# Cross-covariance attention: reading the logits straight from the grams, with a matmul of ones to spread 1/|k|

## The chip, the core and the metric

The kernel runs on one core of one Trainium2 chip. The metric is the device time in microseconds (us) of one execution. The engines are named as in the profile: PE (TensorE), DVE (VectorE), ACT (ScalarE), POOL (GpSimd) and SP, which issues all the transfers here.

## What is computed

```python
batch, heads, seq, dim = 8, 12, 512, 64        # Q, K, V: float32
Q_norm = Q / (np.linalg.norm(Q, axis=-2, keepdims=True) + 1e-10)
K_norm = K / (np.linalg.norm(K, axis=-2, keepdims=True) + 1e-10)
attn = np.einsum('bhnd,bhne->bhde', Q_norm, K_norm)
attn = np.exp(attn - np.max(attn, axis=-1, keepdims=True))
attn = attn / (np.sum(attn, axis=-1, keepdims=True) + 1e-10)
return np.einsum('bhnd,bhde->bhne', V, attn).astype(np.float32)
```

For each of 96 heads the attention matrix is only 64 x 64: columns of Q against columns of K, each column scaled by the inverse of its norm over the 512 rows, then a softmax along the K columns, then V times that matrix.

## The kernel before

The 96 heads are worked on in 24 units of four heads. A unit's Q and K are two float32 tiles of 128 x 1024 (32 partitions to a head). `cast_q` and `cast_k` turn them into one bfloat16 tile `qkb` in which each row holds Q's 64 columns and then K's 64 columns. `grams` multiplies this tile with itself: 64 matmuls, in four row groups of PE, accumulate in PSUM (`gbuf`) for each head a 128 x 128 matrix. Its rows and columns 0 to 63 belong to Q, 64 to 127 to K. The diagonal therefore holds the squared norms, the upper right block Q^T K and the lower left block K^T Q.

`norms` (L115) reads the diagonal with four masked sums on DVE and raises it to the power -1/2 on POOL (L120, tile `rq`: the first 64 partitions hold 1/|q|, the other 64 hold 1/|k|). `keep_kq` (L108) copies K^T Q from PSUM to SBUF on ACT. `scale_k` (L125) multiplies its rows by 1/|k| on POOL. `logits` (L131) transposes the four heads' blocks on PE into the PSUM tile `lg`. `scale_q` (L135) multiplies the rows of the result, which are now Q's columns, by 1/|q| on DVE. `exps` and `normalise` make the softmax, and write the result into one of twelve zeroed bfloat16 tiles `abuf` (memsets at L213).

V goes another way. It is loaded for two units at a time, cast to bfloat16 (`cast_v`, L96), transposed on PE (`vtrans`, L155) and copied out by ACT (L159); the last four units skip the cast and are transposed as float32 (`vtrans_f32`, L170). `doubled` (L176) copies an attention matrix to the other 64 partitions by a matmul with the identity; `dup`, where it writes, shares a PSUM tile with `lg`. `outs` (L188) multiplies the transposed V with two heads' matrices at a time, and L192 copies the products to SBUF, from where SP stores them.

All loads and stores are on SP's queue, in the order in which the program issues them. Q and K have five buffers each, V four. The schedule is manual: what each engine does follows the order of the calls in the loop over s. Stage s issues the load of unit s+3, the grams, norms, copy and scale of unit s, the logits and exponentials of unit s-1 and the normalisation and doubling of unit s-2; the outputs follow at 0.9 units a stage. The PSUM tile of the grams has one buffer, so the grams of unit s+1 wait until the norms and the copy of unit s have read it. After the loop a tail of six steps makes the last six outputs, with the last unit's logits between them:

```python
        if i == 2:
            scale_q(last)
            exps(last)
        ...
        outs(u, both)
        if i == 1:
            logits(last)
```

Of the kernel before, what the change touches and what calls it, by code (L numbers as in the profile page):

```python
# [8 lines left out]
F32 = mybir.dt.float32  # L9
BF16 = mybir.dt.bfloat16  # L10
AF = mybir.ActivationFunctionType
ALU = mybir.AluOpType
AX = mybir.AxisListType

D = 64
HU = 4
# [11 lines left out]
def kernel(  # L28
# [7 lines left out]
    nc = tc.nc  # L36
    B, H, N, _ = Q.shape
# [9 lines left out]
    const = ctx.enter_context(tc.tile_pool(name="const", bufs=1))  # L47
# [6 lines left out]
    small = ctx.enter_context(tc.tile_pool(name="small", bufs=4))  # L54
# [7 lines left out]
    def outs_by(s):  # L62

        return max(0, (s - 2) * 9 // 10)


    qf, kf, vf, vb, qkb, nsq, rq, kqs, sl, ex, vt, so, kq = ({} for _ in range(13))

    def load_qk(u):
        qf[u] = qp.tile([128, R, D], F32, name="qf")  # L70
# [4 lines left out]
    def load_v(w):  # L75
        vf[w] = vp.tile([128, 2 * R * D], F32, name="vf")
        nc.sync.dma_start(out=vf[w], in_=Vf[w])

    def store(u, g=slice(0, SV)):
        nc.sync.dma_start(out=Of[u][:, g], in_=so[u][:, g].rearrange("p s t d -> p s (t d)"))  # L80
# [8 lines left out]
    def cast_v(v):  # L89

        w, i = divmod(v, 2)
        if i == 0:
            vb[w] = vbp.tile([128, A, TP, 2 * D], BF16, name="vb")
        x = vf[w].rearrange("p (a t d) -> p a t d", a=A, d=2 * D)
        for t, copy in ((2 * i, nc.scalar.copy), (2 * i + 1, nc.vector.tensor_copy)):
            copy(vb[w][:, :, t], x[:, :, t])  # L96
# [5 lines left out]
                x = qkb[u][NV * h:NV * (h + 1), t, :]  # L102
                nc.tensor.matmul(gbuf[:, h, 0:2 * D], x, x, start=(t == 0), stop=(t == R - 1), tile_position=(NV * h, 0))  # L103

    def keep_kq(u):

        kq[u] = small.tile([128, HU, D], F32, name="kq")
        nc.scalar.copy(kq[u][D:], gbuf[D:, :, 0:D])  # L108

    def norms(u):  # L110

# [7 lines left out]
        r = rq[u] = small.tile([128, HU], F32, name="rq")  # L119
        nc.gpsimd.tensor_tensor(out=r, in0=n2, in1=mhalf, op=ALU.pow)  # L120

    def scale_k(u):

        kk = kqs[u] = small.tile([128, HU, D], F32, name="kqs")
        nc.gpsimd.tensor_tensor(  # L125
            out=kk[D:], in0=kq[u][D:], in1=rq[u][D:, :, None].to_broadcast([D, HU, D]), op=ALU.mult,
        )

    def logits(u):
        for h in range(HU):  # L130
            nc.tensor.transpose(lg[:, h, :], kqs[u][D:, h, :], ident[D:, D:])  # L131

    def scale_q(u):
        s = sl[u] = small.tile([D, HU, D], F32, name="sl")
        nc.vector.tensor_tensor(out=s, in0=lg, in1=rq[u][0:D, :, None].to_broadcast([D, HU, D]), op=ALU.mult)  # L135

    def exps(u):
        e = ex[u] = small.tile([D, HU, D], F32, name="ex")
        nc.scalar.activation(e, sl[u], AF.Exp)  # L139

    def normalise(u):
        s = small.tile([D, HU], F32, name="esum")
        nc.vector.reduce_sum(out=s, in_=ex[u], axis=AX.X)
        ri = small.tile([D, HU], F32, name="rinv")
        nc.vector.reciprocal(ri, s)
        a = abuf[u % len(abuf)]
        nc.vector.tensor_tensor(out=a[0:D, :, 0, :], in0=ex[u], in1=ri[:, :, None].to_broadcast([D, HU, D]), op=ALU.mult)  # L147

    def vtrans(v):

        w, i = divmod(v, 2)
        ps = ps_v.tile([128, A, 2, 128], BF16, name="vps")
        for t in range(2):
            for a in range(A):
                nc.tensor.transpose(ps[:, a, t, :], vb[w][:, a, 2 * i + t, :], identb)  # L155

        if i == 0:
            vt[w] = vtp.tile([128, TP, 128, A], BF16, name="vt")
        nc.scalar.copy(vt[w][:, 2 * i:2 * i + 2], ps.rearrange("p a t c -> p t c a"))  # L159
# [13 lines left out]
    def doubled(u):  # L173

        a = abuf[u % len(abuf)]
        nc.tensor.matmul(dup[D:], identb[0:D, 0:D], a[0:D, :, 0, :], tile_position=(0, D))  # L176
        nc.scalar.copy(a[D:, :, 1, :], dup[D:])

    def outs(u, copies=(nc.scalar.copy, nc.scalar.copy)):
        s = so[u] = sop.tile([128, SV, TP, 2 * D], F32, name="so")  # L180
        a = abuf[u % len(abuf)]
        v = vt[u // 2][:, :, u % 2 * 64:(u % 2 + 1) * 64]
        for g in range(SV):
            po = ps_o.tile([128, TP, 2 * D], F32, name="po")
            for t in range(TP):
                for x in range(2):
                    h = 2 * g + x
                    nc.tensor.matmul(  # L188
                        po[MV * x:MV * (x + 1), t, :], v[:, t, NP * h:NP * (h + 1), :].rearrange("p c a -> p (c a)"),
                        a[:, h].rearrange("p a d -> p (a d)"), tile_position=(0, MV * x),  # L190
                    )
            copies[g](s[:, g], po)  # L192

    ps_g = main.enter_context(tc.tile_pool(name="ps_g", bufs=1, space=bass.MemoryType.PSUM))
    gbuf = ps_g.tile([128, HU, 512], F32, name="gram")
    ltile = ps_l.tile([128, 2, HU, D], F32, name="lgdup")
    lg = ltile[0:D, 0]
# [6 lines left out]
    ident = const.tile([128, 128], F32, name="ident")  # L204
# [2 lines left out]
    nc.gpsimd.tensor_copy(identb, ident)  # L207
    mhalf = const.tile([128, HU], F32, name="mhalf")
    nc.gpsimd.memset(mhalf, -0.5)
    abuf = []  # L210
    for i in range(12):
        a = const.tile([128, HU, 2, D], BF16, name=f"ab{i}")
# [3 lines left out]
    def on(f, u):  # L216
        if 0 <= u < U:
            f(u)
# [5 lines left out]
    for s in range(U):  # L224
        n0, n1 = outs_by(s - 1), outs_by(s)
        on(load_qk, s + LOAD_AHEAD)
        while nv < min(U, n1 + 5) // 2:
            load_v(nv)
            nv += 1
        while nst < n1 - 3:  # L230
            store(nst)
            nst += 1
        new = range(nt, n1 + 2) if s >= 1 else ()
        for v in new:
            cast_v(v)
        on(cast_q, s + 1)
        on(normalise, s - 2)
        on(grams, s)
        on(norms, s)
        on(keep_kq, s)  # L240
        on(scale_k, s)
        on(logits, s - 1)
        on(scale_q, s - 1)
        on(exps, s - 1)
        on(cast_k, s + 1)
        for v in range(n0, n1):
            outs(v)
        on(doubled, s - 2)
        for v in new:
            vtrans(v)  # L250
            nt = v + 1

    last = U - 1
# [4 lines left out]
    for i, u in enumerate(range(n1, U)):  # L258
        while nv < min(U, u + 6) // 2:
            load_v(nv)  # L260
            nv += 1
        store(u - 3)
        if i == 0:
            normalise(last - 1)
        if i == 2:
            scale_q(last)
            exps(last)
        if i == 3:
            normalise(last)
        on(vtrans_f32, u + 2)  # L270
        if i == 1:
            doubled(last - 1)
        if i == 3:
            doubled(last)
        outs(u, both)
        if i == 1:
            logits(last)
    for u in range(U - 3, last):
        store(u)
    for g in range(SV):  # L280
# [30 lines left out]
```

## Time and profile before

| | |
|---|---|
| time, median of 5 runs | 131.73 us (131.51 to 133.2) |
| profiled execution | 131.73 us, its span 130.0 us |
| busy share of the span | PE 69%, DVE 76%, ACT 65%, POOL 53% |
| DMA | 50.67 MB, mean 390 GB/s |
| mean granted TensorE clock | 0.823 of full speed |

The profile cuts the span in 40 slices of 3.25 us. Its chain of waits is followed back from the last instruction, each step to what released it. In a line of a group, the figures after the first bar are the busy time in us and the mean of one instruction in ns; those after the second are the idle time of the engine just before these instructions, and what ended most of it. In lines of the chain and of the timeline the first two numbers are the start and the length in us. Matrix products read "stationary columns, then moving operand", as "64*64 64x256".

### The profile page before, as it was taken

The numbers are of one execution on the slowest core, as the hardware profiler recorded it, in microseconds if no ns is written. First come the engines' busy times: TensorE is split into PE (matmuls) and PEld (weight loads), VectorE is DVE, ScalarE is ACT, GpSimd is POOL, SyncE is SP. The second block draws the span as 40 slices with busy tenths as digits, with TensorE's granted clock in tenths as the row PEclk, the third lists the DMA queues.
The fourth block names the chain that finished last, engine by engine and source line by source line (L and its number), as shares of the span: only waits on it lengthen the run. The fifth ranks groups of instructions, "written<-read, shape, count | busy, mean of one in ns | idle before, by whom it ended". The sixth has DMA issues, their size and how long they took to land.

```text
span 130.0 us, 5388 instructions
## 1 busy us (share of the span) xinstructions
PE 89.9 (69%) x2232; PEld 69.9 (54%) x2232; DVE 98.7 (76%) x366; ACT 84.8 (65%) x159; POOL 69.1 (53%) x68
## 2 busy tenths in 40 slices
PE   0044736779876988698966997759848966889630
PEld 0043634557655766486844685538627844668410
DVE  0774676898797989595899879797698498878740
ACT  3001375137799889875986379969759849987530
POOL 7924183688357755661588437727617718540000
PEclk9999995555999689655798569995995599999997
DMA  4999999999999999999999999999999999989784
GB/s 153 328 392 434 422 398 411 405 429 393 414 416 403 426 408 407 422 409 409 415 413 409 415 415 420 405 424 413 413 415 416 405 420 417 412 351 340 306 310 184
DMA packets 15208, 50.67 MB, mean 390 GB/s; under 512 B 1360, under 2 KB 1360, under 8 KB 13648
## 3 DMA queue, kind: packets, MB, share of 16 engines
q1 hardware_dynamic: 15184, 50.34, 97.1%
q8 instruction: 17, 0.28, 0.8%
q14 instruction: 7, 0.06, 0.1%
HBM read 37.75 MB, written 12.58 MB: 387 GB/s over the span
## 4 chain that ended last, share of the span: by engine, by line
PE 31%; DMA 26%; DVE 17%; ACT 9%; POOL 7%; issue 4%; SPq 2%; POOLq 0%; ACTq 0%; DVEq 0%
DMA vf<-in_V_dram 18%; PE gram L103 13%; DMA kf<-in_K_dram 9%; DVE scr L115 6%; PE po L188 6%; POOL rq L120 5%; PE vps L155 5%; PE lgdup L131 3%; ACT so L192 3%; PE vps L170 2%; ACT vt L159 2%; PE lgdup L176 2%; DVE qkb L84 2%; DVE qkb L87 2%; DVE sl L135 2%
## 5 line engine op out<-in xcount | busy, mean ns | idle before, releaser
L120 POOL TENSOR_TENSOR rq<-nsq,mhalf 128x4 f32<-128x4 f32 x24 | 47.6, 1983 | 44.0 <-DVE nsq L115 36.0
L103 PE MATMUL gram<-qkb 32*128 32x128 bf16 x1536 | 37.5, 264 | 14.4 <-DVE qkb L87 11.0
L103 PEld LDWEIGHTS <-qkb 32*128 32x128 bf16 x1536 | 31.1, 118 | 21.5 <-DVE qkb L87 14.1
L115 DVE CUSTOM_DVE_ANT_0 scr<-gram,ident 128x128 f32<-128x128 f32 x96 | 22.1, 284 | 11.7 <-PE gram L103 11.6
L108 ACT COPY kq<-gram 64x256 f32<-64x256 f32 x24 | 8.8, 367 | 30.5 <-DVE nsq L115 30.2
L192 ACT COPY so<-po 128x512 f32<-128x512 f32 x42 | 22.8, 588 | 1.6 <-PE po L188 1.0
L84 DVE CAST qkb<-qf 128x1024 bf16<-128x1024 f32 x24 | 19.8, 827 | 4.0 <-DMA qf<-in_Q_dram 4.0
L159 ACT COPY vt<-vps 128x1024 bf16<-128x1024 bf16 x20 | 20.2, 1012 | 1.2 <-PE vps L155 0.7
L188 PE MATMUL po<-ab,vt 128*64 128x128 bf16 x384 | 18.5, 242 | 2.0 <-ACT so L192 0.9
L155 PEld LDWEIGHTS <-vb 128*128 128x128 bf16 x160 | 11.7, 115 | 13.8 <-ACT kq L108 7.9
L155 PE MATMUL vps<-identb,vb 128*128 128x128 bf16 x160 | 15.8, 257 | 2.7 <-ACT vt L159 2.4
L188 PEld LDWEIGHTS <-vt 128*64 128x64 bf16 x384 | 13.5, 121 | 6.5 <-issue 4.0
L87 DVE CAST qkb<-kf 128x1024 bf16<-128x1024 f32 x24 | 16.2, 675 | 0.0
L125 POOL TENSOR_TENSOR kqs<-kq,rq 64x256 f32<-64x256 f32 x24 | 14.9, 621 | 1.9
L131 PE MATMUL lgdup<-ident,kqs 64*64 64x64 f32 x96 | 12.0, 259 | 4.7 <-POOL kqs L125 4.4
L176 PE MATMUL lgdup<-ab,identb 64*64 64x256 bf16 x24 | 7.4, 310 | 11.0 <-DVE sl L135 10.1
L96 ACT CAST vb<-vf 128x512 bf16<-128x512 f32 x20 | 12.3, 621 | 2.4 <-DMA vf<-in_V_dram 2.4
L96 DVE CAST vb<-vf 128x512 bf16<-128x512 f32 x20 | 8.5, 430 | 5.9 <-DMA vf<-in_V_dram 5.9
L131 PEld LDWEIGHTS lgdup<-ident,kqs 64*64 64x64 f32 x96 | 7.5, 128 | 8.9 <-POOL kqs L125 6.5
L139 ACT ACTIVATE ex<-sl 64x256 f32<-64x256 f32 x24 | 10.0, 417 | 2.0 <-DVE sl L135 1.2
L147 DVE TENSOR_TENSOR ab<-ex,rinv 64x256 bf16<-64x256 f32 x24 | 10.4, 432 | 0.8
L135 DVE TENSOR_TENSOR sl<-lgdup,rq 64x256 f32<-64x256 f32 x24 | 9.9, 412 | 1.1 <-PE lgdup L131 0.6
(20 smaller groups left out, 58.0 us busy)
## 6 DMA issues: line engine op xcount, KB each, us to landing
qf<-in_Q_dram SPq DMA_DIRECT2D x24, 512.0 KB, 11.3
kf<-in_K_dram SPq DMA_DIRECT2D x24, 512.0 KB, 11.2
vf<-in_V_dram SPq DMA_DIRECT2D x12, 1024.0 KB, 12.5
out_dram<-so SPq DMA_DIRECT2D x23, 512.0 KB, 11.3
out_dram<-so SPq DMA_DIRECT2D x2, 256.0 KB, 3.3
```

Source lines behind the costliest of these rows:

```text
L84: nc.vector.tensor_copy(qkb[u][:, :, 0:D], qf[u])
L87: nc.vector.tensor_copy(qkb[u][:, :, D:], kf[u])
L96: copy(vb[w][:, :, t], x[:, :, t])
L103: nc.tensor.matmul(gbuf[:, h, 0:2 * D], x, x, start=(t == 0), stop=(t == R - 1), tile_position=(NV * h, 0))
L115: nc.vector.tensor_tensor_reduce(out=scr, in0=gbuf[:, h, 0:2 * D], in1=ident, scale=1.0, scalar=1e-20, op0=ALU.mult, op1=ALU.add, accum_ou ...
L120: nc.gpsimd.tensor_tensor(out=r, in0=n2, in1=mhalf, op=ALU.pow)
L125: nc.gpsimd.tensor_tensor(out=kk[D:], in0=kq[u][D:], in1=rq[u][D:, :, None].to_broadcast([D, HU, D]), op=ALU.mult,)
L131: nc.tensor.transpose(lg[:, h, :], kqs[u][D:, h, :], ident[D:, D:])
L155: nc.tensor.transpose(ps[:, a, t, :], vb[w][:, a, 2 * i + t, :], identb)
L159: nc.scalar.copy(vt[w][:, 2 * i:2 * i + 2], ps.rearrange("p a t c -> p t c a"))
L188: nc.tensor.matmul(po[MV * x:MV * (x + 1), t, :], v[:, t, NP * h:NP * (h + 1), :].rearrange("p c a -> p (c a)"), a[:, h].rearrange("p a d ...
L192: copies[g](s[:, g], po)
```

## The change

The rows of the upper right block, Q^T K, already have the orientation that the softmax wants. `keep_qk` copies this block (partitions 0 to 63) instead of the lower left one. It goes into one of four constant tiles `qk`, whose partitions 64 to 127 hold an identity matrix for each head, written once at the start. `scale` multiplies all 128 partitions by `rq`: the upper half becomes Q^T K with its rows times 1/|q|, the lower half diagonal matrices of 1/|k|. `spread_k` multiplies a 64 x 64 block of ones with these diagonal matrices on PE, in float32, so that every row of `lg` holds 1/|k| along its columns. `logits` is now the elementwise product of `lg` and the scaled Q^T K on DVE. The four transposes are gone; in the order of the calls `spread_k` stands where `logits` stood, and `logits` where `scale_q` stood. At the start POOL writes the block of ones and the four identity tiles, ahead of the twelve memsets.

```diff
-    def keep_kq(u):
-
-        kq[u] = small.tile([128, HU, D], F32, name="kq")
-        nc.scalar.copy(kq[u][D:], gbuf[D:, :, 0:D])
+    def keep_qk(u):
+
+        nc.scalar.copy(qk[u % len(qk)][0:D], gbuf[0:D, :, D:2 * D])
...
-    def scale_k(u):
-
-        kk = kqs[u] = small.tile([128, HU, D], F32, name="kqs")
-        nc.gpsimd.tensor_tensor(
-            out=kk[D:], in0=kq[u][D:], in1=rq[u][D:, :, None].to_broadcast([D, HU, D]), op=ALU.mult,
-        )
+    def scale(u):
+
+        x = sc[u] = small.tile([128, HU, D], F32, name="sc")
+        nc.gpsimd.tensor_tensor(out=x, in0=qk[u % len(qk)], in1=rq[u][:, :, None].to_broadcast([128, HU, D]), op=ALU.mult)
+
+    def spread_k(u):
+
+        nc.tensor.matmul(lg, ones[D:], sc[u][D:], tile_position=(D, 0))
 
     def logits(u):
-        for h in range(HU):
-            nc.tensor.transpose(lg[:, h, :], kqs[u][D:, h, :], ident[D:, D:])
-
-    def scale_q(u):
         s = sl[u] = small.tile([D, HU, D], F32, name="sl")
-        nc.vector.tensor_tensor(out=s, in0=lg, in1=rq[u][0:D, :, None].to_broadcast([D, HU, D]), op=ALU.mult)
+        nc.vector.tensor_tensor(out=s, in0=lg, in1=sc[u][0:D], op=ALU.mult)
...
+    ones = const.tile([128, D], F32, name="ones")
+    nc.gpsimd.memset(ones, 1.0)
+    qk = []
+    for i in range(4):
+        x = const.tile([128, HU, D], F32, name=f"qk{i}")
+        nc.gpsimd.tensor_copy(x[D:], ident[D:, None, D:].to_broadcast([D, HU, D]))
+        qk.append(x)
     abuf = []
...
-        on(keep_kq, s)
-        on(scale_k, s)
+        on(keep_qk, s)
+        on(scale, s)
+        on(spread_k, s - 1)
         on(logits, s - 1)
-        on(scale_q, s - 1)
         on(exps, s - 1)
...
         if i == 2:
-            scale_q(last)
+            logits(last)
             exps(last)
...
         if i == 1:
-            logits(last)
+            spread_k(last)
```

More of the change, by code (lines that the diff above doesn't have):

```diff
@@ L64, in outs_by @@
         return max(0, (s - 2) * 9 // 10)
-    qf, kf, vf, vb, qkb, nsq, rq, kqs, sl, ex, vt, so, kq = ({} for _ in range(13))
+    qf, kf, vf, vb, qkb, nsq, rq, sc, sl, ex, vt, so = ({} for _ in range(12))
     def load_qk(u):
```

## The prediction

> **What bounds the kernel now.** I read the page's slices first, then its queues, then the chain of waits, then the timeline where the chain turns.
>
> ```profile
> PEclk9999995555999689655798569995995599999997
> DMA  4999999999999999999999999999999999989784
> GB/s 153 328 392 434 422 398 411 405 429 393 414 416 403 426 408 407 422 409 409 415 413 409 415 415 420 405 424 413 413 415 416 405 420 417 412 351 340 306 310 184
> ...
> q1 hardware_dynamic: 15184, 50.34, 97.1%
> ```
>
> From slice 3 to slice 35 the DMA engines are full at some 413 GB/s. A unit moves half a MB each of Q, K, V and output: 2.10 MB / 413 GB/s = 5.08 us of DMA. Per unit DVE is busy 98.7 / 24 = 4.1 us and PE 89.9 / 24 = 3.7 us. So up to about 104 us the transfers set the pace. In the last five slices the rate falls to 340, then 184: there the transfers wait for computation. Where one turns into the other stands in the chain of waits:
>
> ```profile
> 91.16 12.47 DMA vf<-in_V_dram
> 103.65 0.43 DVE vb L96
> ...
> 106.99 2.25 POOL rq L120
> 109.31 0.62 POOL kqs L125
> 109.98 0.41 PE lgdup L131 x4
> 110.39 0.57 PE po L188 x16
> ...
> 117.86 0.36 PE lgdup L131 x4
> 118.22 1.02 PE vps L170 x8
> ```
>
> At 103.65 VectorE stops waiting for V (it had sat idle 1.68 us for it). From there to the last copy, whose 0.69 us begin at 124.86, no step of the chain is a DMA. So what the change costs is read from these 22 us; before them a stage has 1 us to spare on DVE and the last wait forgives 1.68 us. The span is 130.0 us and this execution took 131.73, so 1.73 us lie around the span; 131.73 is also the median, so a sum against this execution is one against the median.
>
> **The change, part by part.**
>
> ```profile
> L155 PE MATMUL vps<-identb,vb 128*128 128x128 bf16 x160 | 15.8, 257 | 2.7 <-ACT vt L159 2.4
> L125 POOL TENSOR_TENSOR kqs<-kq,rq 64x256 f32<-64x256 f32 x24 | 14.9, 621 | 1.9
> L131 PE MATMUL lgdup<-ident,kqs 64*64 64x64 f32 x96 | 12.0, 259 | 4.7 <-POOL kqs L125 4.4
> L176 PE MATMUL lgdup<-ab,identb 64*64 64x256 bf16 x24 | 7.4, 310 | 11.0 <-DVE sl L135 10.1
> L135 DVE TENSOR_TENSOR sl<-lgdup,rq 64x256 f32<-64x256 f32 x24 | 9.9, 412 | 1.1 <-PE lgdup L131 0.6
> ```
>
> *Copy on ScalarE* (L108, 367 ns): the same 64x256 float32 from the same PSUM tile, other partitions and columns. Zero.
>
> *Multiply on VectorE* (L135, 412 ns): the same form; its second operand is a full 64x256 tile rather than a broadcast. It reads PSUM plus one SBUF operand before and after. Zero.
>
> *Scale on GpSimd* (L125): 64 partitions become 128, 256 elements in each. No row shows such a multiply on 128. The low end is the row, 0.62 us; the high end is time growing with partitions, 1.24 us. The Trainium skill (GPSIMD Engine Reference, Architecture) gives each of eight cores its own 16 partitions, all running the same instruction, which makes it 0.62 again. I take 0.62: zero. It is on the chain once, at 109.31; the other two late ones end at 112.27 and 115.64, before PE asks at 113.03 and 117.84. The high end thus costs 0.62 us once.
>
> *Matmul on PE.* Four float32 transposes of 64 columns go; one float32 matmul of 256 columns comes. The groups' means mix clocks, so I use the fastest instructions, as the tail runs at granted clock 1.00 from 112 us. In bfloat16, 128 columns take 213 ns (L103's minimum) and 256 take 265 ns (L176's): 0.41 ns a column on a fixed 0.16 us. In float32, transposes of 64 and 128 columns take 213 and 272 ns (minima of L131 and L170): 0.92 ns a column, twice as much. No float32 product stands in the trace. Three prices, with 256 columns:
> - as bfloat16 (the row of L176): 0.27 us;
> - at the rate of the float32 transposes: 0.16 + 256 x 0.92 ns = 0.39 us;
> - the Trainium skill (FP8 and Floating Point Precision, TensorE Precision Notes) speaks against the change: a true float32 product needs four passes through the array, every pairing of high and low halves. Estimate: 0.16 + 4 x 256 x 0.41 ns = 0.58 us; with three further weight loads uncovered, at 104 ns (L131's shortest), 0.89 us.
>
> The pieces in the chain are 0.41 us at 109.98 (unit 21) and 0.36 us at 117.86 (unit 23): 0.77 together. Two spreads cost 0.54, 0.78, 1.16 or 1.78 us, so the end moves by -0.23, 0.0, **+0.39** or +1.01. By the row nearest in shape the kernel gains a little; by the rule it loses. I take four passes, since [...] the row of L176 is not float32. Unit 22's spread (113.03) lies beside its norms: VectorE reads the result only at 113.72, and 113.03 + 0.58 = 113.61. It is covered by 0.1 us; at 0.89 it would cost 0.2 more.
>
> Queued behind the spread on PE are the output matmuls, the doubling matmul, the V transposes and the next grams. The doubling also waits for the VectorE multiply (10.1 us of L176's idle time), which comes after the norms: 0.84 us of norms and 0.41 of multiply against 0.58 + 0.64 of spread and output matmuls. These just match, so at full clock no new wait arises. Before, the weight load waited for GpSimd; now the weights are the constant ones and only the product waits. I give nothing for that.
>
> At half clock a spread is dearer: L176's slowest is 420 ns, L103's 310, so 0.86 ns a column on 0.20 us, and four passes make 1.08 us against some 0.63 for four transposes, +0.45 in a stage. Between 20 and 104 us the DMA's 5.08 us hide it; without that cover, see the third rival.
>
> *Prologue on GpSimd.*
>
> ```profile
> 1.64 5.59 POOL L213 MEMSET ab<- 128x512 bf16 x12
> 3.96 3.81 DVE L84 CAST qkb<-qf 128x1024 bf16<-128x1024 f32 x1 [3.96 <-DMA qf<-in_Q_dram]
> 10.46 0.33 SPq L72 DMA_DIRECT2D qf<-in_Q_dram  x1
> 11.71 0.33 SPq L73 DMA_DIRECT2D kf<-in_K_dram  x1
> 14.18 0.76 DVE L96 CAST vb<-vf 128x512 bf16<-128x512 f32 x2 [2.15 <-DMA vf<-in_V_dram]
> ```
>
> The first cast takes 3.81 us where a median one takes 0.68, and ends half a microsecond after GpSimd's last memset: it is held up by GpSimd. Ahead of those memsets the change puts one memset of 128x64 (0.15 us between the rows of 102 and 204 ns) and four copies of 64x256. A copy of 128x128 (L207) took 289 ns, so 256 elements take 0.48 us by the slope, four 1.9 us: 2.1 us in all. The cast then ends near 9.9 instead of 7.8 us and the first gram starts near 10.5. VectorE's wait for V, 2.15 us before 14.18, takes up its part; PE's second gram ends near 16 instead of 14 us and V's transposes come 1 to 2 us late. The loads don't feel it: the sixth Q load, which needs the first cast's buffer, goes out at 10.46[...]; the sixth K load at 11.71, and its cast now ends near 10.6. SP's order is unchanged. Later stages regain the delay at 1 us each. Cost at the end: zero; if none were regained, 2.1.
>
> **Sum:** 131.73 + 0.39 = 132.1 us.
>
> **Rivals.**
> 1. *The spread streams like one bfloat16 pass.* For it: L176 has its shape. Against: every float32 row here is twice as dear. 131.73 - 0.23 = 131.5 us.
> 2. *The wait for GpSimd grows, or weight loads stay uncovered.* For: PE sat idle 1.27 us before 109.98 waiting for this very scale. Against: 0.62 us for 64 partitions fits a cost by elements. 132.1 + 0.62 = 132.7; with uncovered loads, 131.73 + 1.01 = 132.7 as well.
> 3. *PE becomes the bound while its clock is low; slower than before.* Half-clock pieces in the chain add up to 0.63 + 1.00 + 0.35 + 0.96 + 1.85 = 4.8 us a stage; with 0.9 output units a stage, 4.6. A spread of 1.08 makes that 5.05, just under the DMA's 5.08: this is the point from which it decides. With two weight loads uncovered (0.2 us each at half clock) a stage takes 5.45; over the 13 low slices (42 us, 8 stages) 3.0 us are lost, less the 1.68 forgiven; the same loads (0.1 us each at full clock) make the two late spreads 1.57 us, 0.80 over the transposes: 131.73 + 1.3 + 0.8 = 133.8 us. Against: a low clock here goes with an idle PE, and a busier PE should see less of it.
> 4. *The late reciprocal root lands better.* rq (L120) takes 1.0 to 2.7 us, longer where VectorE casts beside it. The one of 2.25 on the chain could fall to 1.25: 132.1 - 1.0 = 131.1. It could as well be longer.
>
> **How the numbers follow.** The forecast has 0.60 (its own range 131.4 to 132.9), rival 1 has 0.12, rival 2 0.10, rival 3 0.13, rival 4 0.05. The range 130.9 to 133.9 takes in the first, second and fourth, and the third's middle. About 1% (1.3 us) is what a measurement of this kernel can tell from no change. Above 133.05 lie most of rival 3 and the upper edges of the forecast and of rival 2: 0.18. Below 130.4 only a lucky rival 4 with rival 1: 0.04. Within 1%: 0.78.
>
> **What the next profile would show.** The spread, 24 products of 256 columns (or 96 passes of them), together near 0.58 us at full clock and 1.1 at half; over 0.9 at full clock my price is wrong. The GpSimd scale near 0.62 us on 128 partitions. The first cast ending near 9.9 us. DMA still at 413 GB/s to 104 us, with VectorE idle for V before it. The last copy about 0.4 us later. If SP's loads wait for casts or PE, or the rate dips before slice 33, the claim that transfers hide everything before the tail is wrong.

## The result and the profile after

The changed kernel takes 1.0026 of the time of the kernel before (95% interval 1.0003 to 1.0048), which is 0.34 us (0.04 to 0.63) of 131.7. The median of all its runs is 132.87 us (131.43 to 136.58), of all runs of before in the same comparison 132.55 us (130.92 to 135.64). The ratios of this document compare only the runs within 1.5% of the fastest of their kernel, which leaves out the execution that was profiled (134.29 us, span 132.5): in it PE ran at half clock for 6.8 us of the tail, so its steps are compared below where the clock is full.

The slices of the changed kernel (granted PE clock, DMA share, GB/s):

```profile
PEclk9999999999999599999997579999985698559995
DMA  4999999999999999999999999999999999955775
GB/s 156 364 383 427 436 396 408 412 412 409 414 413 401 429 402 412 429 398 412 418 404 413 418 419 411 407 424 409 407 425 409 416 412 410 396 218 224 263 271 207
```

As before, the transfers are full up to slice 35. Then the rate is lower than it was (218 to 271 GB/s against 306 to 351, and 207 against 184 in the last slice); it falls just behind the 35th and 36th slices, in which the clock is at 5. The groups of the new instructions (operands and count, then busy us and mean ns, then idle time before them and its releaser):

```profile
L128 PE MATMUL lgdup<-sc,ones 64*64 64x256 f32 x48 | 19.2, 488 | 6.4 <-POOL sc L124 6.3
L124 POOL TENSOR_TENSOR sc<-qk,rq 128x256 f32<-128x256 f32 x24 | 15.8, 656 | 1.9
L132 DVE TENSOR_TENSOR sl<-lgdup,sc 64x256 f32<-64x256 f32 x24 | 9.9, 413 | 2.6 <-PE lgdup L128 2.1
```

A float32 spread is two instructions (48 for 24 units), not one and not four. GpSimd's scale has twice the partitions and nearly the same mean; its median is 612 ns against 611. The chain of waits in the tail:

```profile
103.52 0.43 DVE vb L96
...
106.86 2.26 POOL rq L119
109.19 0.62 POOL sc L124
109.85 0.64 PE lgdup L128 x2
...
111.84 1.78 PE gram L103 x64
113.62 1.05 PE lgdup L128 x2
...
120.38 0.59 PE lgdup L128 x2
...
122.64 0.68 DVE so L189
```

In the chain of before the same grams and the same copy on VectorE are

```profile
111.81 1.03 PE gram L103 x64
...
119.89 0.68 DVE so L192
```

The last V comes at 103.52, as it came at 103.65, and the wait for GpSimd is where it was. The two spreads at full clock take 0.64 and 0.59 us where the transposes took 0.41 and 0.36. From the start of the first piece to the next grams it is 1.99 us where it was 1.83, and from the second to the copy on VectorE 2.26 where it was 2.03: 0.39 us more in all. Between them lies the half clock: grams of 1.78 us where they took 1.03, and a third spread, unit 22's, of 1.05 us on the chain.

### The profile page after: what moved, and what is told of

Read it like the earlier page. It is cut to its first block, busy times and chain, and to the rows that moved or that the text cites. A ratio compares the mean times of both kernels' runs of the same rounds, so it can differ in the third digit from the quotient of the medians.

```text
span 132.5 us, 5249 instructions
## 1 busy us (share of the span) xinstructions
PE 93.4 (71%) x2184; PEld 64.9 (49%) x2184; DVE 98.0 (74%) x366; ACT 81.6 (62%) x159; POOL 71.4 (54%) x73
## 4 chain that ended last, share of the span: by engine, by line
PE 33%; DMA 26%; DVE 22%; POOL 6%; issue 5%; ACT 3%; SPq 2%; POOLq 0%; ACTq 0%
DMA vf<-in_V_dram 17%; PE gram L103 12%; DMA kf<-in_K_dram 8%; DVE scr L114 6%; PE lgdup L128 6%; PE po L185 5%; PE vps L152 5%; POOL rq L119 4%; PE vps L167 3%; DVE sl L132 3%; DVE qkb L87 3%; DVE qkb L84 3%; PE lgdup L173 2%; DVE vb L96 2%; DVE ab L144 2%
## 5 line engine op out<-in xcount | busy, mean ns | idle before, releaser
L119 POOL TENSOR_TENSOR rq<-nsq,mhalf 128x4 f32<-128x4 f32 x24 | 46.4, 1934 | 42.3 <-DVE nsq L114 30.9
L103 PE MATMUL gram<-qkb 32*128 32x128 bf16 x1536 | 34.6, 252 | 15.7 <-DVE qkb L87 11.0
L103 PEld LDWEIGHTS <-qkb 32*128 32x128 bf16 x1536 | 28.9, 112 | 23.9 <-DVE qkb L87 16.2
L107 ACT COPY qk<-gram 64x256 f32<-64x256 f32 x24 | 8.8, 366 | 32.9 <-DVE nsq L114 32.0
L128 PE MATMUL lgdup<-sc,ones 64*64 64x256 f32 x48 | 19.2, 488 | 6.4 <-POOL sc L124 6.3
L84 DVE CAST qkb<-qf 128x1024 bf16<-128x1024 f32 x24 | 18.6, 776 | 5.5 <-DMA qf<-in_Q_dram 5.5
L124 POOL TENSOR_TENSOR sc<-qk,rq 128x256 f32<-128x256 f32 x24 | 15.8, 656 | 1.9
L152 PE MATMUL vps<-identb,vb 128*128 128x128 bf16 x160 | 14.9, 247 | 2.0 <-ACT vt L156 2.0
L132 DVE TENSOR_TENSOR sl<-lgdup,sc 64x256 f32<-64x256 f32 x24 | 9.9, 413 | 2.6 <-PE lgdup L128 2.1
L128 PEld LDWEIGHTS lgdup<-sc,ones 64*64 64x64 f32 x48 | 5.4, 157 | 10.4 <-POOL sc L124 8.3
```

The source lines that it names most:

```text
L84: nc.vector.tensor_copy(qkb[u][:, :, 0:D], qf[u])
L124: nc.gpsimd.tensor_tensor(out=x, in0=qk[u % len(qk)], in1=rq[u][:, :, None].to_broadcast([128, HU, D]), op=ALU.mult)
L128: nc.tensor.matmul(lg, ones[D:], sc[u][D:], tile_position=(D, 0))
```

## The experiments

Theory: the change costs what the two late spreads add on PE, 0.46 us in this chain, and everything before 104 us is hidden. Rivals: the prologue, GpSimd, or PE's extra work in the body. All ratios are to the kernel before.

**1. More of the late spreads.**

```diff
-        nc.tensor.matmul(lg, ones[D:], sc[u][D:], tile_position=(D, 0))
+        for _ in range(4 if u in (21, 23) else 1):
+            nc.tensor.matmul(lg, ones[D:], sc[u][D:], tile_position=(D, 0))
```

> The changed kernel with the spreads of units 21 and 23 issued four times in place of once (same result). Theory: each further one costs 0.43 us of PE on the chain, six of them 2.6 us: about 2.9 us above before. Rival (the end waits for something else, stores or VectorE): below 1 us above before.

1.019 (1.007 to 1.031), 2.5 us, from two of six runs; the median of all six is 4.6 us above that of all runs of before (137.41 against 132.84). The size is therefore poorly known; the low end of the interval, 0.9 us, just touches the rival. The chain shows the first four spreads, full width:

```profile
108.99 1.89 PE lgdup L129 x8
```

1.89 us for four, 1.25 more than the one of 0.64. So what is added to a late spread reaches the end. In this execution the second four (118.33) are not on the chain, which there goes through a store; so place by place only the first is shown.

**2. More spreads in the body.**

```diff
+        for _ in range(2 if u < 20 else 1):
+            nc.tensor.matmul(lg, ones[D:], sc[u][D:], tile_position=(D, 0))
```

> The changed kernel with the spread of units 0 to 19 issued twice (same result). Theory (transfers hide PE's work before the tail): 20 further products of 0.43 us at full and 0.85 at half clock, 9 to 17 us of PE, cost nothing: as the changed kernel, some 0.35 us above before. Rival (PE is or becomes the bound in the body): PE's stage of 4.6 us plus 0.45 and 0.85 exceeds the DMA's 5.08 us where the clock is half: 3 us or more above before.

1.0167 (1.0098 to 1.0236), 2.2 us slower, from six runs (the medians of all runs differ by 1.6 us): the theory's "costs nothing" fell, and the result lies between the two, nearer to the rival. The clock is not to blame, as this profile has the highest mean of all, 0.937. The waits show where the time goes:

```profile
DVE sl L133 <- PE lgdup L129: 5.4, 10, 1.1
...
DVE vb L96 <- DMA vf<-in_V_dram: 2.0, 1, 2.0
```

VectorE waited four times for V in the kernel before (5.9 us in all); here it does so once, at the start, and instead waits ten times for a spread. The spread as the change has it fits under the transfers (VectorE still waits 1.52 us for the last V); one more per unit does not. The cover in the body is thus less than what one more spread takes, 0.43 us at full and 0.85 at half clock.

**3. A longer prologue.**

```diff
         qk.append(x)
+        for _ in range(2):
+            nc.gpsimd.tensor_copy(x[D:], ident[D:, None, D:].to_broadcast([D, HU, D]))
```

> The changed kernel with each of the four identity tiles written three times on GpSimd at the start: eight further copies, 0.36 us each by the changed kernel's profile, 2.9 us. Theory (VectorE's wait for V and the full DMA queue take the start up): as the changed kernel, some 0.35 us above before. Rival (the start is passed on to the end): 2 to 3 us above before.

0.9993 (0.9952 to 1.0034), nothing within half a microsecond. GpSimd's last memset begins at about 14 us and the first reciprocal root at 14.68 instead of 11.59 us, and the last V comes at 103.65 as before. The prologue costs nothing that these runs resolve, even with three times the copies. That a kernel with more work than the changed one comes out 0.3% below it also shows how little weight the +0.34 us can bear.

**4. A cheaper spread in all units, twice.**

```diff
-        x = sc[u] = small.tile([128, HU, D], F32, name="sc")
+        x = sc[u] = small.tile([128, HU, D], BF16, name="sc")
...
-    ones = const.tile([128, D], F32, name="ones")
+    ones = const.tile([128, D], BF16, name="ones")
```

> The scaled tile and the ones are bfloat16, so the spread is a single product of bfloat16; nothing else changes (1/|k| and the scaled logits are rounded to bfloat16). Theory (the two late spreads on PE's chain are what the change costs): a late spread takes 0.27 us instead of 0.64, against 0.41 and 0.36 us of the transposes, so about 0.2 us under before and 0.7 under the changed kernel. Rival (the cost comes from the prologue or from GpSimd's scale of 128 partitions): no gain over the changed kernel, still some 0.35 us above before.

> The kernel with bfloat16 spreads in all units once more, because its first runs came out 1.3% above before with an interval of 0.6 to 2.0%. If that was the luck of where PE's half-clock windows and the last V transfer fell, it comes out within 0.5% of before. If less PE work in the body really costs time, it is 1% above again.

1.0132 (1.0062 to 1.0203), and again 1.0213 (1.0160 to 1.0266), six runs each. By the medians of all runs it is 0.6% and 1.5% above before, so the kernel is slower, but by how much is uncertain. Yet the late spread is as cheap as foreseen. The chain of the first:

```profile
108.94 1.85 PE gram L103 x59
...
119.50 0.22 PE lgdup L128
```

0.22 us in place of 0.59. What was saved, and more, came back elsewhere. PE stood idle for 2.45 us before 107.71, behind a doubling that waits for VectorE, which waits for the last V (0.54 us in the changed kernel). The next grams ran at half clock. In two windows of this execution (the first number behind the window's length is PE's busy time, the third from the end its granted clock):

```profile
104.50:107.90 3.40, 0.95 (x18) 0.58 (x17) 3.33 (x15) 1.09 (x3) 0.50 (x1) 1.00 1.04 422
107.90:111.30 3.40, 3.36 (x78) 2.72 (x79) 2.69 (x11) 3.05 (x6) 2.77 (x2) 0.50 1.04 418
```

The last V itself was cast at 104.47 (at 104.37 in the second profile), 0.7 to 0.8 us later than before; why is open. None of this was in the theory.

**5. The cheaper spread for the last three units only**, the float32 one for units 0 to 20 (the scaled tile and the ones in bfloat16 where u >= 21).

> The changed kernel with the scaled tile and the ones in bfloat16 for units 21 to 23 alone; every earlier unit as in the changed kernel. Theory (the late spreads cost, and PE's work in the body is hidden): the spreads of units 21 and 23 take 0.27 us in place of 0.64 and 0.59, so about 0.2 us below before. Rival (a bfloat16 spread is slower for another reason, as the first run of it in all units suggests): 1% or more above before, as that run.

1.0024 (0.9991 to 1.0056): none of the loss of experiment 4, but not the 0.2 us below before either; that value, 0.9985, lies just outside the interval. The last spread did save what it should:

```profile
118.98 0.22 PE lgdup L128
...
120.87 0.68 DVE so L189
```

That is 1.89 us from the spread to the copy, against 2.26 in the changed kernel and 2.03 before. The first was not worth its 0.37 us in this profile: PE is at half clock there, the spread ends at 110.78, and VectorE's multiply, which comes after the norms, starts only at 111.34. With the last spread's 0.37 us alone, +0.34 would become about 0, which the interval allows.

**6. Cheap spreads, but PE kept as busy.** Experiment 4's kernel with

```diff
+        for _ in range(4 if u < 21 else 1):
+            nc.tensor.matmul(lg, ones[D:], sc[u][D:], tile_position=(D, 0))
```

> The kernel with bfloat16 spreads in all units, each spread of units 0 to 20 issued four times, so that PE is busy with it for as long as with the float32 spread; units 21 to 23 once (same result). Theory (PE work in the body keeps the clock up, and taking it out is what made the bfloat16 kernel 1.3 to 2.1% longer than before): this comes back to the kernel with late bfloat16 spreads only, within 0.5% of before. Rival (something else in bfloat16 spreads, such as explicit weight loads or the bfloat16 operand on VectorE, costs time): 1% or more above before.

1.0002 (0.9975 to 1.0029). With sixty-three superfluous products the ratio to before is 1.3 to 2.1% lower than without them (0.9 to 1.8% by the medians of all runs). This excludes the bfloat16 operand and the explicit weight loads as the cause of experiment 4: all are still there. It is the PE work that counts. Of the 22 runs one took more than 133 us, of before's 51 in the same comparison 20. The mean granted clock over all runs was 0.875 and 0.856 in the two of experiment 4 and 0.884 here, but 0.877 to 0.879 in the kernel before, which is as fast as this one: the mean over a whole run does not tell the kernels apart.

**7. Output matmuls ahead of the spread in stage 22, alone and with experiment 5's edit.**

```diff
+        if s != 22:
             on(spread_k, s - 1)
             on(logits, s - 1)
             on(exps, s - 1)
...
         for v in range(n0, n1):
             outs(v)
+        if s == 22:
+            on(spread_k, s - 1)
+            on(logits, s - 1)
+            on(exps, s - 1)
```

> The changed kernel with, in stage 22 alone, the output matmuls and their copies ahead of the spread, logits and exponentials of unit 21. Theory (in that stage PE's queue stands 1.3 us behind a spread that waits for GpSimd): the output matmuls, 0.57 us, run in this wait, so about 0.2 us below before, 0.57 below the changed kernel. Rival (the wait moves to the doubling matmul, which needs VectorE's multiply in any case): no change against the changed kernel.

> Late spreads in bfloat16 and the output matmuls first in stage 22. Theory: both add up, 0.7 and 0.57 us below the changed kernel, so some 0.8 us (0.6%) below before. Rival (they overlap, as the wait for GpSimd bounds that stage): 0.4 us below before or less.

1.0047 (1.0014 to 1.0080) and 1.0036 (1.0002 to 1.0071). The 0.57 us were not gained. In the first, PE now waits 0.51 us at the doubling (111.95) for VectorE's multiply: the rival's wait is there. (PE is at half clock in this stage, so the profile shows the wait, not its size at full clock.)

**8. Filling PE's idle time before the tail.** In the changed kernel (ten products behind the grams of unit 22, four behind those of unit 21), in the kernel before, and, with eight and twelve, in the kernel of experiment 6:

```diff
+    def fill(s, n):
+        for _ in range(n):
+            nc.tensor.matmul(dup[D:], identb[0:D, 0:D], abuf[(s - 3) % 12][0:D, :, 0, :], tile_position=(0, D))
...
         on(grams, s)
+        if s in (21, 22):
+            fill(s, 10 if s == 22 else 4)
```

> The changed kernel with idle PE time filled: small bfloat16 products into the part of PSUM that the doubling overwrites later, four behind the grams of unit 21 and ten behind those of unit 22, where PE waits 1.3 us for GpSimd (same result). Theory (the tail's length is set by PE's granted clock there, and idle PE before it lowers the clock): the runs with a late half-clock stretch become fewer, the median over all runs falls by 0.5 to 1 us, the fastest runs stay as they are. Rival (the clock there is luck, or filler of 1 us is too little): median and spread as for the changed kernel, or longer by what the filler delays.

> The kernel before with the same filler at units 21 and 22. Theory: fewer runs with a late half-clock stretch, its median over all runs 0.5 to 1 us below before, fastest runs unchanged. Rival: as before, or longer by the filler.

> The kernel with bfloat16 spreads issued four times for units 0 to 20, and filler as well: twelve small products behind the grams of unit 21, where PE stands up to 3 us behind VectorE's wait for the last V, and eight behind those of unit 22 (same result). Theory (idle PE in that wait lowers the clock for the tail): 0.3 to 0.5% below before, hardly a run above 133 us. Rival (what that kernel gained came from the body alone, and filler here only delays): as that kernel, equal to before, or above it by up to 1%.

0.9955 (0.9919 to 0.9991), 1.0022 (0.9990 to 1.0054) and 0.9993 (0.9953 to 1.0033). Only the first is below before, by 0.6 us, and it is the one version here that beats both kernels. I would not lean on it: its interval only just clears 1, it is the best of twelve kernels, and the same filler did nothing for the kernel before. By the medians of all runs the three lie 0.4 us below, 0.3 above and 1.4 below before, against a foreseen 0.5 to 1 below for the first two; more than 133 us took 4 of 14, 10 of 23 and 1 of 14 runs (before: 20 of 51 for the first two, 10 of 19 for the third). So the third did not become 0.3 to 0.5% faster in the ratio, but "hardly a run above 133 us" came true. Its profile shows a tail at full clock. The windows from 104 to 118 us of before and of this one; the three last columns are PE's granted clock, the DMA share and GB/s:

```profile
104.00:118.00 14.00, 10.52 (x279) 8.28 (x272) 12.31 (x49) 11.42 (x23) 6.69 (x6) 0.98 0.98 389
```

```profile
104.00:118.00 14.00, 12.58 (x284) 9.79 (x277) 12.62 (x49) 10.89 (x22) 6.71 (x6) 0.99 0.99 396
```

| profiled execution | last V to last copy, us | clock, 104 to 118 us |
|---|---|---|
| filler in the kernel of experiment 6 | 103.18 to 124.16: 20.98 | 0.99 |
| before | 103.65 to 124.86: 21.21 | 0.98 |
| experiment 6 | 104.16 to 125.65: 21.49 | 0.88 |
| experiment 5 | 104.04 to 125.85: 21.81 | 0.76 |
| experiment 4, first | 104.47 to 126.36: 21.89 | 0.86 |
| experiment 3 | 103.65 to 125.64: 21.99 | 0.88 |
| experiment 7, with late bfloat16 | 103.96 to 126.56: 22.60 | 0.72 |
| experiment 7, alone | 104.00 to 127.39: 23.39 | 0.76 |
| changed kernel | 103.52 to 127.62: 24.10 | 0.74 |
| experiment 4, second | 104.37 to 129.03: 24.66 | 0.61 |
| filler in the changed kernel | 103.39 to 128.53: 25.14 | 0.63 |
| filler in the kernel before | 104.15 to 129.45: 25.30 | 0.63 |

Each is one execution, so the table compares tails, not kernels (experiments 1 and 2, which lengthen the spreads, are left out). A tail is longer where the clock in it is lower: the column spans 4.3 us, two late spreads more or less are 0.5. The same tail, instruction for instruction, took 21.99 and 24.10 us (experiment 3 and the changed kernel), and 21.89 and 24.66 (experiment 4). The mean clock does not fix the length, though: at 0.76 there are 21.81 and 23.39 us, so it also matters which steps the half clock meets. The last V moves by 1.3 us.

When does the clock fall? In the fourteen profiles it keeps its value for 3.41 us or a multiple of that (3.4, 6.8, 10.2 us and so on). Cut into pieces of 3.41 us, the spans hold 291 pieces at full clock. In 37 of them PE was busy for less than half of the time, and 36 of these were followed by half clock; in 163 it was busy for 70% or more, and none was. Between these shares it goes either way: the changed kernel's piece from 108.4 us (busy 63%, PE waiting there for GpSimd) was followed by half clock, that of before from 107.9 us (62%) was not. From half clock it came back after 43 of 52 pieces in which PE was busy all the time, and after none of the 19 in which it was busy for less than 85%. Twelve of the fourteen profiles have a fall of the clock behind a piece that starts between 100 and 113 us. Before's own profile and that of the third filler are the two without.

## Why the prediction held, point by point

*The place.* The body is hidden by the transfers and the tail pays: the last V came 0.13 us earlier, and from 40 to 104 us the changed kernel moves 412 to 413 GB/s, where it was 412 to 414. Experiment 1 shows that late spreads reach the end.

*The price of a spread.* 0.58 us was predicted from four passes and 1.08 at half clock; 0.59 to 0.64 and 1.04 to 1.11 were measured. Four passes was the right price, in the form of two instructions at twice bfloat16's time a column: in experiment 1 a further spread costs 1.25 / 3 = 0.42 us, 0.21 an instruction and 0.81 ns a column, against 0.41 in bfloat16. That is near the rate of the float32 transposes, but paid twice. Rival 1, a single bfloat16 pass, is out. One reading was wrong without harm: the weight load does not run ahead of GpSimd's scale, although its weights are the constant ones. At 109.85 it starts with the product, once the scale is done. The spread behind that wait took 0.64 us and the one without a wait 0.59, so at most 0.05 us of weight loads shows; that half of rival 2 is out.

*GpSimd.* 612 ns (median) on 128 partitions against 611 on 64, and 0.62 us on the chain: the other half of rival 2 is out too. The late reciprocal root took 2.26 us where it took 2.25, so rival 4 did not occur in this profile.

*The prologue.* Its price was too high (four copies took 1.43 us, not 1.9) and its path was wrong. The start of the changed kernel:

```profile
1.84 1.43 POOL L212 COPY qk<-ident 64x256 f32<-64x256 f32 x4
3.34 6.73 POOL L217 MEMSET ab<- 128x512 bf16 x12
3.99 0.88 DVE L84 CAST qkb<-qf 128x1024 bf16<-128x1024 f32 x1 [3.99 <-DMA qf<-in_Q_dram]
7.81 2.81 DVE L84 CAST qkb<-qf 128x1024 bf16<-128x1024 f32 x1 [1.47 <-DMA qf<-in_Q_dram]
```

The first cast was not held up to 9.9 us; it took 0.88 us, the memsets were stretched instead (6.73 us for twelve against 5.59), and the cast that stood behind them is the one at 7.81. The first norms began at 10.54 us, against 10.50 before. The conclusion, that nothing reaches the end, holds in experiment 3 for three times the copies.

*The cover of unit 22's spread.* It was put at 0.1 us. In the profiled execution, at half clock, the spread is on the chain (1.05 us). At full clock it held in experiment 1's profile, where this spread ends at 113.98 and the multiply starts at 114.21. It did not in experiment 3's, where the spread waited for GpSimd's scale until 113.58 and was on the chain.

*The sum.* Predicted +0.39 us; the chain's two spreads add 0.46; the ratio gives +0.34 (0.04 to 0.63). These agree, but the agreement is not a proof of the one cause, and the stated range would have held no change at all as well. The experiments that took the late cost out again (5 and 7) did not give the 0.7 and 0.57 us back. What the prediction did not have is the clock of the tail. It took 1.00 there from one profile, one of the two among fourteen that keep it, and treated the spread's price as the only thing that the change does to PE. That the rest came to nothing on balance is luck as far as the prediction goes. Experiments 4 and 6 show that PE work has a second effect, of the other sign: where work is taken out of the body, the kernel gets slower. So the net +0.34 us is likely a sum of at least two terms of both signs, and how it divides stays open. That a PE that is idle for more than half of 3.41 us is followed by half clock is shown by the pieces counted above. That the whole second effect runs through this clock is still argued; no run held the clock fixed, and in experiment 4 the last V came later too.

*The third rival* (PE as the bound in the body) did not occur, but stood closer than thought: one more spread a unit brings it about.

## What to carry to other kernels

Price a new instruction by the nearest row of the same type and engine, and find the stage where the transfers cease to be the bound: only there is the price paid. Count also what the edit does to PE's busy share in the microseconds before that stage, since a shorter PE job that leaves it idle can cost more than it saves, here most likely through the clock. When executions of one kernel differ by more than the effect, read the effect from steps at equal clock and leave its division open.

## What the runs showed that was not expected

- Superfluous PE work paid: bfloat16 spreads in all units gave 1.0132 and 1.0213, the same spreads issued four times in the body 1.0002.
- The same tail took 21.99 us at a mean granted clock of 0.88 and 24.10 at 0.74, and in the bfloat16 kernel 21.89 at 0.86 and 24.66 at 0.61.
- PE busy for less than half of a 3.41 us piece was followed by half clock in 36 of 37 cases, busy for 70% or more in none of 163.
- The two kernels with four bfloat16 spreads a unit are no faster than before at their best, but took more than 133 us in only 1 of 22 and 1 of 14 runs (before: 20 of 51 and 10 of 19).
- GpSimd's memsets and VectorE's casts hold each other up in either order: 3.81 us for a cast behind memsets before, 6.73 us for twelve memsets with casts between them after.
